# Moving the streamed weights' five places into a pool of their own, ahead of the working tiles

## The chip, the cores and the metric

The kernel runs on one NeuronCore of one Trainium2 chip. The metric is the device time of the whole program in microseconds (us), as the median of several runs; the profile is one further execution, taken by the hardware profiler.

## The reference

One layer of a hybrid decoder trunk over 4,096 tokens of width 1,024, in float32. One projection of the tokens gives 28 groups of 128 columns for five branches and a gate; the gated branches go through an output projection, and a layer norm closes the layer:

```python
proj = x @ w_in
xa, ba, ca, u, v, xc, da, dg, q, gate = jnp.split(proj, SPLIT_OFFSETS, axis=-1)
y_a = short_gated_conv(xa, ba, ca, conv_a_w)
y_b = spatial_gating(u, v, sg_ln_g, sg_ln_b, sg_w, sg_b)
y_c = multiscale_pool(xc, pool_w, pool_scale)
y_d = conformer_conv(da, dg, cc_dw_w, cc_dw_b, cc_ln_g, cc_ln_b, cc_pw_w)
y_e = memory_cross_attention(q, mem, w_kv)
h = jnp.concatenate([y_a, y_b, y_c, y_d, y_e], axis=-1) * jax.nn.silu(gate)
x = layer_norm(DEEPNORM_ALPHA * x + h @ w_out, ln_g, ln_b)
```

## The kernel before

**Order of the work.** The 4,096 tokens are eight blocks of 512, taken as four pairs (the loop over `p`). For a pair, `x_prep` (L121) loads the transposed tokens and makes seven combinations of the pair's x quarters, each in two halves of the contraction; each is split by `split_to` (L85) into a rounded high part (ScalarE) and the rest (VectorE), since every large product is done as three products of float32r splits. Then fourteen calls of `mpair` (L225) each make two groups of 128 columns for both blocks by seven half-size products, a Strassen scheme. One such product, `product` (L205), is 12 matmuls: four chunks of the contraction, and for each the three lines L209 (w high by x low), L211 (w low by x high) and L212 (w high by x high). The weights are the stationary operand, 128 by 128, the x tile the moving one, 128 by 512. The results are combined by VectorE (L90) and ScalarE (L236), and between the calls the branches' work is issued: convolutions, pooling, norms, attention. The 31-tap convolution of a pair (L462) is spread by `take(conv, ...)` over the first calls of the next pair.

**The streamed weights.** Each of the seven weight combinations of a call is a tile of 1,024 float32 a partition (both splits of half the contraction), taken with tag "ws": 5 places of 4,096 bytes. In the first pair `w_first` makes them and stores them to DRAM (L184); in the other pairs `w_again` (L199) loads them again (L202), 512 KB each, by the SyncE queue. `ready(5)` (L217) keeps five places in use: one is read, four are ahead. A load waits until the product before has freed its place.

**The output projection.** After the last pair, the split output weights `wo` and the norm's rows take 22 of the 28 places of the x tiles. `load_h` (L713) brings the gated branches for a unit of 256 tokens and splits them into five stationary tiles named h. For an even unit all five lie in x places; for an odd unit the first four lie in "ws" places and the fifth in an x place:

```python
        def part(j):
            if u % 2 == 0 or j == 4:
                return xc.tile([P, 2 * T], F32R, tag=htags[j if u % 2 == 0 else 5], name=nm("h"))
            return tt("ws", F32R, n="h")
```

A unit is two groups of 128 tokens, each 60 matmuls at L757 (10 chunks, 3 split products, 2 halves of the columns), so 120 matmuls; there are 16 units. Of an odd unit's 120 matmuls, 96 read a stationary tile in a "ws" place. VectorE adds the residual, takes the statistics and applies the norm (L760 to L770).

**The memory.** The pools lie one behind the other in each partition's memory, in the order in which they are opened. In the compiled kernel before: constants (`cp`) from byte 1,152; the 28 places of 4,096 bytes of the x tiles (`xc`) from 19,712 to 134,400; the working tiles (`tp`) from 134,400; small tiles (`sp`) from 225,664. Within `tp` the tags stand in the order of their first use: cc (8 × 2,048 bytes), raw (4 × 4,096), big (5 × 4,224), ss (2 × 2,048), ws (5 × 4,096, from 192,384 to 212,864), wk (4 × 2,176), st (2 × 2,048). The pointwise weights of the conformer branch, two tiles of `cp`, lie at 2,272 and 4,320; they are the stationary tiles of the matmuls at L485 to L487.

Of the kernel before, what the change touches and what calls it, by code (L numbers as in the profile page):

```python
# [18 lines left out]
P = 128  # L19
# [33 lines left out]
def trunk(ctx, tc, a, out):  # L53
    nc = tc.nc
    cp = ctx.enter_context(tc.tile_pool(name="cp", bufs=1))
    xc = ctx.enter_context(tc.tile_pool(name="xc", bufs=1))
    tp = ctx.enter_context(tc.tile_pool(name="tp", bufs=4))
    sp = ctx.enter_context(tc.tile_pool(name="sp", bufs=4))
    pm = ctx.enter_context(tc.tile_pool(name="pm", bufs=4, space=bass.MemoryType.PSUM))
# [4 lines left out]
    def nm(s):  # L64
        uid[0] += 1
        return f"{s}_{uid[0]}"
# [4 lines left out]

    def tt(tag, dt=F32, n=None):
        cols, bufs = SLOTS[tag]
        return tp.tile([P, cols], dt, tag=tag, name=nm(n or tag), bufs=bufs)

    def const(shape, src=None, dt=F32):
        t = cp.tile(shape, dt, name=nm("c"), tag=nm("ct"))
# [43 lines left out]
    def x_prep(p):  # L121
# [8 lines left out]
        def load(kap, j, n):  # L130
            tag = "big" if p == 0 and kap == 1 else "raw"
            raw = tt(tag, n="xraw")[:, :2 * T].rearrange("p (k t) -> p k t", k=2)
            k0 = 4 * j + 2 * kap
            nc.sync.dma_start(out=raw, in_=a["xT"][:, k0:k0 + 2, (2 * p + n) * T:(2 * p + n + 1) * T])
            raws[kap, j, n] = raw
# [32 lines left out]
    def w_first(mp, raws=None):  # L168

        m1, m2 = MPAIRS[mp]  # L170
        if raws is None:
            raws = []
            for m in (m1, m2):
                raw = tt("raw", n="wraw").rearrange("p (k c) -> p k c", k=NK)
                nc.sync.dma_start(out=raw, in_=a["w_in"][m])
                raws += [raw[:, :4], raw[:, 4:]]
        a11, a12, a21, a22 = raws
        s = tt("ss", n="ws0").rearrange("p (k c) -> p k c", k=4)

        def put(i, src):  # L180
            w = tt("ws", F32R, n="w")
            v = w.rearrange("p (s k c) -> p s k c", s=2, k=4)
            split_to(v[:, 0], v[:, 1], src)
            nc.sync.dma_start(out=wd[mp][i], in_=w.bitcast(F32))  # L184
            return v

        yield put(PA, a11)
        add(s, a21, a22)
        yield put(PT1, s)
        sub(s, s, a11)  # L190
        yield put(PT2, s)
        yield put(PB, a12)
        sub(a21, a11, a21)
        yield put(PT3, a21)
        sub(s, a12, s)
        yield put(PD, s)
        yield put(PT4, a22)
# [634 lines left out]
```

## Time and profile before

| | us |
|---|---|
| median of 3 runs | 1,802.05 |
| lowest, highest | 1,799.92, 1,803.36 |
| the profiled execution | 1,802.25 |
| its span, first to last instruction | 1,800.5 |
| mean granted TensorE clock in it | 0.992 of full |

The profile puts TensorE's matmuls (PE) and weight loads (PEld) in two rows, though one engine runs both; a matmul's end is modelled, and consecutive matmuls overlap in it, so their mean time is longer than the spacing of their starts. DVE is VectorE, ACT is ScalarE, POOL is GpSimd, SP is SyncE, whose queue (SPq) issues the DMAs. "L757" is line 757 of the kernel. A busy share is an average; which wait ends last in a stretch is read from the waits of that stretch.

### The profile page before, as it was taken

The numbers are of one execution on the slowest core, as the hardware profiler recorded it, in microseconds if no ns is written. First come the engines' busy times: TensorE is split into PE (matmuls) and PEld (weight loads), VectorE is DVE, ScalarE is ACT, GpSimd is POOL, SyncE is SP. The second block draws the span as 40 slices with busy tenths as digits, with TensorE's granted clock in tenths as the row PEclk, the third lists the DMA queues.
The fourth block names the chain that finished last, engine by engine and source line by source line (L and its number), as shares of the span: only waits on it lengthen the run. The fifth ranks groups of instructions, "written<-read, shape, count | busy, mean of one in ns | idle before, by whom it ended". The sixth has DMA issues, their size and how long they took to land.

```text
span 1800.5 us, 21764 instructions
## 1 busy us (share of the span) xinstructions
PE 1754.9 (97%) x7912; PEld 1383.6 (77%) x7912; DVE 1336.9 (74%) x2461; ACT 507.0 (28%) x937; POOL 44.8 (2%) x87
## 2 busy tenths in 40 slices
PE   5999999999999999999999999999989999999997
PEld 4887777878877787887778788777768888888786
DVE  8678887799966539997643999766379996665665
ACT  4323644420144423013532411354141010000300
POOL 0000000000100001010000000000000000000000
PEclk9999999999999999999999999999989999999999
DMA  7767455776744467675346766544683344332621
GB/s 276 274 239 261 183 198 196 280 238 208 235 163 137 133 217 270 201 230 177 129 151 211 269 201 213 197 143 141 205 289 99 119 132 141 127 100 79 213 71 47
DMA packets 128091, 332.79 MB, mean 185 GB/s; under 512 B 14064, under 2 KB 36080, under 8 KB 127984
## 3 DMA queue, kind: packets, MB, share of 16 engines
q1 hardware_dynamic: 127984, 331.39, 54.3%
q8 instruction: 63, 1.03, 0.2%
q14 instruction: 44, 0.36, 0.1%
HBM read 238.02 MB, written 93.32 MB: 184 GB/s over the span
## 4 chain that ended last, share of the span: by engine, by line
PE 91%; DVE 5%; DMA 2%; ACT 1%; issue 1%; SPq 0%; DVEq 0%; ACTq 0%
PE mm L757 24%; PE mm L209 19%; PE mm L212 19%; PE mm L211 19%; PE ax L632 3%; PE ax L607 2%; DVE xl L87 2%; PE ax L627 2%; DMA xraw<-in_xT 1%; DVE xraw L93 1%; PE ax L577 1%; PE ax L428 1%; PE ax L485 0%; PE ax L475 0%; PE ax L487 0%
## 5 line engine op out<-in xcount | busy, mean ns | idle before, releaser
L209 PE MATMUL mm<-xl,w 128*128 128x512 f32 x1568 | 627.4, 400 | 25.9 <-DVE xl L87 20.3
L211 PE MATMUL mm<-xh,w 128*128 128x512 f32 x1568 | 624.6, 398 | 0.9 <-DVE w L87 0.9
L212 PE MATMUL mm<-xh,w 128*128 128x512 f32 x1568 | 623.2, 398 | 0.0
L757 PE MATMUL mm<-wo,h 128*128 128x512 f32 x1920 | 445.8, 394 | 7.8 <-DVE h L87 7.8
L757 PEld LDWEIGHTS mm<-wo,h 128*128 128x128 f32 x1920 | 362.6, 189 | 87.6 <-DVE h L87 8.6
L209 PEld LDWEIGHTS mm<-xl,w 128*128 128x128 f32 x1568 | 297.1, 189 | 98.6 <-DVE xl L87 24.4
L212 PEld LDWEIGHTS mm<-xh,w 128*128 128x128 f32 x1568 | 296.8, 189 | 70.6 <-issue 3.6
L211 PEld LDWEIGHTS mm<-xh,w 128*128 128x128 f32 x1568 | 297.2, 190 | 68.2 <-issue 2.4
L462 DVE SCALAR_TENSOR_TENSOR acc<-din,c,acc 128x1024 f32<-128x1024 f32 x240 | 303.8, 1279 | 0.6 <-ACT acc L459 0.2
L86 ACT CAST h<-hraw 128x1024 fp32r<-128x1024 f32 (+1 forms) x48 | 43.3, 910 | 319.8 <-PE mm L757 235.3
L90 DVE TENSOR_TENSOR cc<-mm,v 128x512 f32<-128x512 f32 x112 | 76.8, 688 | 68.8 <-PE mm L212 68.3
L760 DVE SCALAR_TENSOR_TENSOR r<-r,mm 128x512 f32<-128x512 f32 x64 | 43.5, 687 | 79.8 <-PE mm L757 79.7
L86 ACT CAST xh<-xraw 128x1024 fp32r<-128x1024 f32 x56 | 57.9, 1051 | 64.2 <-DVE xraw L93 41.5
L90 DVE TENSOR_TENSOR t<-mm,t 128x512 f32<-128x512 f32 x56 | 38.6, 689 | 49.9 <-PE mm L212 49.9
L87 DVE TENSOR_TENSOR xl<-xraw,xh 128x1024 fp32r<-128x1024 f32 x56 | 66.7, 1221 | 11.3 <-ACT xh L86 11.1
L388 ACT ACTIVATE cc<-cc 128x512 f32<-128x512 f32 x44 | 27.9, 634 | 157.2 <-DVE cc L90 157.0
L87 DVE TENSOR_TENSOR h<-hraw,h 128x1024 fp32r<-128x1024 f32 (+1 forms) x48 | 49.7, 1041 | 26.3 <-issue 13.1
L236 ACT COPY t<-mm 128x512 f32<-128x512 f32 x56 | 32.9, 587 | 128.6 <-PE mm L212 128.5
L611 DVE TENSOR_REDUCE mx<-ax 128x2 f32<-128x512 f32 x64 | 42.7, 682 | 30.2 <-PE ax L607 29.9
L90 DVE TENSOR_TENSOR cc<-mm,t 128x512 f32<-128x512 f32 x56 | 38.5, 688 | 35.6 <-PE mm L212 35.1
L615 ACT ACTIVATE e<-ax,mx 128x256 f32<-128x256 f32 x128 | 59.3, 476 | 17.1 <-DVE mx L611 16.2
L435 ACT ACTIVATE nrm<-ax,nmr,rs 128x256 f32<-128x256 f32 x64 | 30.7, 570 | 115.9 <-DVE nmr L433 115.9
(147 smaller groups left out, 1531.8 us busy)
## 6 DMA issues: line engine op xcount, KB each, us to landing
w<-wd SPq DMA_DIRECT2D x294, 512.0 KB, 3.9
wd<-w SPq DMA_DIRECT2D x98, 512.0 KB, 2.9
xraw<-in_xT SPq DMA_DIRECT2D x32, 512.0 KB, 5.5
h<-cc SPq DMA_DIRECT2D x64, 256.0 KB, 3.1
hraw<-h SPq DMA_DIRECT2D x32, 512.0 KB, 4.1
r<-in_x SPq DMA_DIRECT2D x64, 256.0 KB, 3.0
out<-r SPq DMA_DIRECT2D x64, 256.0 KB, 2.0
wraw<-in_w_in SPq DMA_DIRECT2D x22, 512.0 KB, 4.3
```

The lines of the kernel that those rows point to most:

```text
L86: nc.scalar.copy(out=hi, in_=src)
L87: nc.vector.tensor_tensor(out=lo, in0=src, in1=hi.bitcast(F32), op=ALU.subtract)
L90: nc.vector.tensor_tensor(out=dst, in0=x, in1=y, op=ALU.add)
L209: nc.tensor.matmul(out=ps, lhsT=w[:, 0, k], rhs=xl[:, r], start=start and k == 0, stop=False, skip_group_check=True)
L211: nc.tensor.matmul(out=ps, lhsT=w[:, 1, k], rhs=xh[:, r], start=False, stop=False, skip_group_check=True)
L212: nc.tensor.matmul(out=ps, lhsT=w[:, 0, k], rhs=xh[:, r], start=False, stop=stop and k == 3, skip_group_check=True)
L462: nc.vector.scalar_tensor_tensor(out=accs[i], in0=dins[i][:, k:k + 2 * T], scalar=dww[:, i, k:k + 1], in1=accs[i], op0=ALU.mult, op1=ALU.add)
L611: nc.vector.tensor_reduce(out=mx, in_=sc[j], axis=AX.X, op=ALU.max, negate=True)
L615: nc.scalar.activation(out=e[:, c], in_=sc[j][:, c], func=AF.Exp, bias=mx[:, c:c + 1], accum_out=su[:, c:c + 1])
L632: nc.tensor.matmul(out=po[64 * j:64 * j + 64], lhsT=vm[:, mc, 64 * hd:64 * hd + 64], rhs=pT, start=(mc == 0), stop=(mc == 1))
L757: nc.tensor.matmul(out=ps[n], lhsT=l[:, P * (c % 2):P * (c % 2) + P], rhs=ww[:, T * n:T * n + T], start=(k == 0 and l is lo), stop=(k == N ...
L760: nc.vector.scalar_tensor_tensor(out=r[n], in0=r[n], scalar=ALPHA, in1=ps[n], op0=ALU.mult, op1=ALU.add)
```

## The change

The tag "ws" leaves the pool `tp` for a pool `wp`, opened between `xc` and `tp`. The tiles, their number, their size and the order of the instructions in the source stay as they are.

```diff
     xc = ctx.enter_context(tc.tile_pool(name="xc", bufs=1))
+    wp = ctx.enter_context(tc.tile_pool(name="wp", bufs=5))
     tp = ctx.enter_context(tc.tile_pool(name="tp", bufs=4))
...
     def tt(tag, dt=F32, n=None):
         cols, bufs = SLOTS[tag]
-        return tp.tile([P, cols], dt, tag=tag, name=nm(n or tag), bufs=bufs)
+        return (wp if tag == "ws" else tp).tile([P, cols], dt, tag=tag, name=nm(n or tag), bufs=bufs)
```

## Rows read from the trace of the kernel before

**Rows 1.** The page: span, and busy us (share of the span) of two engines.
```profile
span 1800.5 us, 21764 instructions
PE 1754.9 (97%) x7912; PEld 1383.6 (77%) x7912; DVE 1336.9 (74%) x2461; ACT 507.0 (28%) x937; POOL 44.8 (2%) x87
```

**Rows 2.** The page: the chain that ended last, share of the span by engine.
```profile
PE 91%; DVE 5%; DMA 2%; ACT 1%; issue 1%; SPq 0%; DVEq 0%; ACTq 0%
```

**Rows 3.** TensorE's waits: who waited for whom, us in total, times, longest.
```profile
PE mm L209 <- DVE xl L87: 20.3, 9, 7.6
PE mm L757 <- DVE h L87: 7.8, 2, 6.7
PE mm L209 <- DVE t L90: 4.8, 3, 3.4
```

**Rows 4.** Groups by line, 1395.5 to 1422.5 us (even unit): count | busy, mean ns | idle before.
```profile
L757 PE MATMUL mm<-wo,h 128*128 128x512 f32 x121 | 27.6, 389 | 0.0
L757 PEld LDWEIGHTS mm<-wo,h 128*128 128x128 f32 x120 | 22.5, 188 | 4.7
```

**Rows 5.** Groups by line, 1422.7 to 1449.7 us (the odd unit behind it).
```profile
L757 PE MATMUL mm<-wo,h 128*128 128x512 f32 x118 | 27.5, 394 | 0.0
L757 PEld LDWEIGHTS mm<-wo,h 128*128 128x128 f32 x117 | 22.0, 188 | 5.1
```

**Rows 6.** Windows, a later even unit and the odd one behind it (columns in rows 12).
```profile
1505.50:1532.50 27.00, 27.00 (x121) 22.37 (x120) 16.53 (x44) 3.79 (x4) 0.00 (x0) 1.00 0.40 130
1532.70:1559.70 27.00, 27.00 (x119) 21.95 (x118) 16.42 (x43) 1.67 (x2) 0.00 (x0) 1.00 0.37 116
```

**Rows 7.** Groups by line, PEld, 376 to 466 us (products of the second pair).
```profile
L212 PEld LDWEIGHTS mm<-xh,w 128*128 128x128 f32 x130 | 24.5, 188 | 5.8
L211 PEld LDWEIGHTS mm<-xh,w 128*128 128x128 f32 x129 | 24.3, 188 | 5.6
L209 PEld LDWEIGHTS mm<-xl,w 128*128 128x128 f32 x129 | 24.3, 188 | 5.7
```

**Rows 8.** Instructions of L486 (conformer's pointwise product): duration ns min/median/max, first and last start.
```profile
L486 PE MATMUL ax<-zz,c x32: 390/395/398, 507.3 to 1691.3; 128*128 128x512 f32 x32
```

**Rows 9.** The page's costliest groups: one of the product's three lines.
```profile
L209 PE MATMUL mm<-xl,w 128*128 128x512 f32 x1568 | 627.4, 400 | 25.9 <-DVE xl L87 20.3
```

**Rows 10.** Groups by line, 0 to 60 us: the same line.
```profile
L209 PE MATMUL mm<-xl,w 128*128 128x512 f32 x31 | 15.4, 495 | 16.7 <-DVE xl L87 13.3 <-DVE t L90 3.4
```

**Rows 11.** Windows: behind the first boundary between pairs, and at the second (columns in rows 12).
```profile
371.00:375.00 4.00, 4.00 (x12) 3.16 (x11) 2.70 (x3) 1.05 (x1) 0.00 (x0) 0.60 0.62 218
690.00:698.00 8.00, 6.49 (x27) 4.73 (x26) 8.00 (x8) 2.94 (x3) 0.00 (x0) 1.00 0.43 132
```

**Rows 12.** Windows: convolution stretches of the second to fourth pair, start of the output projection.
```profile
core 0: us, PE busy (x) PEld busy (x) DVE busy (x) ACT busy (x) POOL busy (x), PEclk, DMA share, GB/s
...
375.00:497.00 122.00, 122.00 (x527) 98.85 (x526) 118.12 (x134) 13.84 (x22) 10.55 (x14) 1.00 0.70 229
...
700.00:820.00 120.00, 120.00 (x522) 97.14 (x521) 115.77 (x134) 13.85 (x22) 10.28 (x14) 1.00 0.70 231
...
1024.00:1142.00 118.00, 118.00 (x510) 95.47 (x509) 114.45 (x130) 13.84 (x22) 10.54 (x14) 1.00 0.71 229
...
1338.00:1485.00 147.00, 147.00 (x632) 120.45 (x631) 144.78 (x267) 17.35 (x19) 0.00 (x0) 0.98 0.41 132
```

**Rows 13.** DMA issue of the streamed weights (KB, median us to landing), and SyncE's waits before it.
```profile
w<-wd SPq DMA_DIRECT2D x294, 512.0 KB, 3.9
...
SPq L202 <- PE mm L212: 661.7, 272, 9.6
```

## The prediction

> **What bounds the kernel now.** I read the page's busy table first, then the chain that ended last, then TensorE's waits, and last the spacing of its matmuls in stretches where it waits for nothing. TensorE is busy for 1,754.9 of the span's 1,800.5 us [rows 1], and 91% of the chain runs on it [rows 2]. Its three largest waits, all for VectorE, add up to 20.3 + 7.8 + 4.8 = 32.9 us, nearly all for the splits at the start and between pairs of blocks [rows 3]. So what counts is how fast matmul follows matmul, and the change can matter only there or in a wait that it makes longer.
>
> The spacing can be read from the weight loads: one LDWEIGHTS stands before each matmul, so its busy time and the idle time before it, added up and divided by the count, give one period. The output projection offers a clean comparison, because it goes through units of 120 matmuls whose stationary half-splits h lie by turns in two places: all in the pool of the x tiles for an even unit (`load_h`, L713), and for an odd unit four of five parts in the "ws" places. All else is the same. An even unit gives (22.5 + 4.7) / 120 = 226.7 ns [rows 4], an odd one (22.0 + 5.1) / 117 = 231.6 ns [rows 5]. Later units repeat it: 121 matmuls touch 27 us of an even one, 119 of an odd one, at full clock in both [rows 6]. Only 96 of an odd unit's 120 matmuls read a "ws" place, so one of those costs 226.7 + 4.9 × 120 / 96 = 232.8 ns. The products of the input projection, whose weights all stream through the "ws" places, give (24.5 + 5.8 + 24.3 + 5.6 + 24.3 + 5.7) / 388 = 232.5 ns [rows 7]: the same slow spacing. The LDWEIGHTS itself takes 188 ns everywhere; only the pause behind it grows, from 39 to 44 ns. So a stationary tile in a "ws" place costs TensorE about 5.8 ns a matmul, whatever the phase of the kernel.
>
> What is special about these places is their address. Before "ws", the pool tp holds 8 × 2,048 + 4 × 4,096 + 5 × 4,224 + 2 × 2,048 = 57,984 bytes, which is 226.5 × 256: the five "big" tiles of 4,224 bytes push "ws" 128 bytes off a multiple of 256, where the x pool's places lie. The places are also high, from 192,384 up, while the fast ones end at 134,400. Position off the multiple, or height: no row parts these two for sure. A third stationary tile speaks for the first: the pointwise weights of the conformer branch lie low (2,272 and up) but 224 bytes off, and their matmuls have the slow length, median 395 ns [rows 8], against 389 for the even units and 394 for the odd [rows 4, 5].
>
> **The change, part by part.** It adds, removes and reorders no instruction and no DMA. The pool wp is opened behind xc, so I expect the five places at 134,400 to 154,880: on a multiple of 256 like the x tiles, directly behind them. On either reading of the address this is the fast side, since 134,400 is a multiple of 256 and the height is next to the fastest places known. The tags cc, raw, big and ss move up by 20,480, which is 80 × 256, so they keep their position relative to 256; wk, st and the small pool stay where they are.
>
> Term 1, the products: 3 × 1,568 = 4,704 matmuls [rows 9]. In the first 60 us TensorE waits for splits and weights anyway; 3 × 31 of them are there [rows 10] and count nothing. That leaves 4,611 × (232.5 − 226.7) = 26.7 us. Term 2, the output projection: eight odd units × 120 × 4.9 ns = 4.7 us. Together 31.4 us.
>
> From this comes what other engines don't let through. Between pairs of blocks TensorE waits for x splits that VectorE works off without a break (8.00 of 8 us [rows 11]). TensorE comes there earlier by what it saves on the last two output groups, 168 matmuls × 5.8 ns = 1.0 us, while part of VectorE's chain starts earlier with it; I charge 0.7 us at three such places, 2.1 us. Then come three stretches in which VectorE is nearly full with the 31-tap convolution: it is busy for 118.1 of 122, 115.8 of 120 and 114.5 of 118 us [rows 12]. TensorE's gain there is about 525 × 5.8 ns = 3.0 us a stretch, and VectorE's room is 3.5 to 4.2 us, so it just fits; I charge 0.5 us each, and 0.5 us for the start of the output projection, where VectorE has 2.2 us of room in 147 us [rows 12] and TensorE gains about 1.5 us. That is 2.0 us. Net: 31.4 − 2.1 − 2.0 = 27.3 us.
>
> The streamed loads stay hidden: a transfer lands 3.9 us after its issue, and the queue's wait before it is for TensorE to free a place [rows 13]; four products of 12 × 226.7 ns lie between, 10.9 us, instead of 11.2. If that cover were gone a late load would cost up to its 3.9 us; it isn't. VectorE's and ScalarE's operands move too, at unchanged position relative to 256; I cost that at nothing, since neither engine is where the chain runs, and allow it 1 us either way in the range.
>
> The profiled execution took 1,802.25 us (span 1,800.5), and the median of the runs is 1,802.05; the sum is made against the first, 1,802.25 − 27.3 = 1,774.9, which against the median is 1,774.7. I take 1,774.8.
>
> A page speaks against all of this. The Trainium skill, "SBUF — State Buffer", section "Who interferes with whom", has the only contention in the lock of the port pair that VectorE and GpSimd share, gives TensorE two independent read ports, and says that "PE and ACT never wait on anyone". By that the place of a tile would be free, and the gain 0 instead of 27.3 us. The trace disagrees as far as the place goes: 226.7 against 231.6 ns between units that differ in nothing else.
>
> **The rivals.** (a) VectorE takes it back. Where it is nearly full, TensorE's gain turns into waits: the three convolution stretches lose 9.0 us and the start of the output projection 1.5, the boundaries 2.1. In addition the granted clock, whose mean was 0.60 in the 4 us after the waits of the first boundary but 1.00 at the second [rows 11], could fall at two more boundaries if their waits grow; 0.60 means 3.2 of the 4 us at the lower of its two levels, 1.2 instead of 2.4 GHz, which costs 1.6 us each time. The time is then 1,802 − 31.4 + 9.0 + 1.5 + 2.1 + 3.2 = 1,786.4. For it: the thin room. Against it: the room exists, and most of it is waiting for TensorE. (b) No change, 1,802: the pool lands elsewhere than I think, or what is slow is a height whose border lies below 154,880, or the streaming itself. Against the last: odd units are slow and stream nothing into these places. (c) Slower: at its new place the stream of transfers lands next to the x tiles, which no transfer writes today. If transfers there hold up TensorE's reads of the moving x tile by as much as the place does now, 5.8 ns, and the weights gain nothing, each product step goes to 238.3 ns and the time to 1,802 + 26.7 = 1,829; it decides from the point at which that cost is larger than the 5.8 ns gained. Against it: the slow spacing is the same in the products, with a DMA share of 0.70 [rows 12], as in odd units, with one of 0.37 [rows 6].
>
> **How the numbers follow.** The forecast, 1,768 to 1,781, has 0.70: its lower end is the full 31.4 us and some 2 us for uncertain spacing. Rival (a), 1,781 to 1,788, has 0.14, rival (b) 0.10, rival (c) 0.06. A range to 1,787 takes in the forecast and most of (a), about 0.82. A measurement of this kernel can tell about 0.2%, 3.6 us, from no change. Forecast and (a) are both faster by more than that: 0.84. Within it lies (b), 0.10, and above it (c), 0.06.
>
> **What the profile after would show.** Right: products and odd units at 226 to 227 ns by the weight loads' rows, matmul means of 389 ns, 121 matmuls in 27 us of every unit, and VectorE's idle time in the convolution stretches shrunk. For (a): the same spacing, but waits of TensorE for VectorE's adds or accumulators that weren't there. For (b): still 232 ns. For (c): spacing above 233 ns that follows the transfers' share. The prediction is wrong if the spacing falls and the time doesn't, or if the spacing stays.

## The result, and the profile after

The changed kernel takes **1,778.58 us**, the median of four runs (1,775.03 to 1,779.4), against 1,802.68 us for the kernel before in the same session (1,799.92 to 1,803.36). The ratio is 0.9865, with a 95% interval from 0.9848 to 0.9882: it is faster by 24.1 us, where 27.3 had been forecast. The profiled execution took 1,778.75 us, 23.5 less than the profiled one of before. In the compiled kernel the five places lie from 134,400 to 154,880, and cc, raw, big and ss have moved up by 20,480. TensorE's 7,912 instructions stand in the same order as before. Line numbers after L56 are one higher, so L209 is now L210 and L757 is L758.

The page of the changed kernel: span, busy time, the chain by engine, two of the costliest groups, and the issue of the streamed loads. They answer to [rows 1, 2, 9, 13].

```profile
span 1777.0 us, 21764 instructions
...
PE 1728.5 (97%) x7912; PEld 1379.6 (78%) x7912; DVE 1334.4 (75%) x2461; ACT 506.6 (29%) x937; POOL 46.2 (3%) x87
...
PE 87%; DVE 7%; DMA 3%; issue 1%; ACT 1%; SPq 0%; DVEq 0%; ACTq 0%
...
L210 PE MATMUL mm<-xl,w 128*128 128x512 f32 x1568 | 620.4, 396 | 27.5 <-DVE xl L88 21.3
...
L758 PE MATMUL mm<-wo,h 128*128 128x512 f32 x1920 | 439.8, 391 | 7.5 <-DVE h L88 7.5
...
w<-wd SPq DMA_DIRECT2D x294, 512.0 KB, 3.8
```

TensorE's busy time fell by 26.4 us with the same 7,912 matmuls, the span by 23.5. So nearly everything happened inside "busy": that row hides spacing, and a reader who looks for idle time only sees nothing. The loads land 3.8 us after their issue, against 3.9 before.

TensorE's waits in the changed kernel: us in total, times, longest; against [rows 3].

```profile
PE mm L210 <- DVE xl L88: 21.3, 12, 7.4
PE mm L758 <- DVE h L88: 7.5, 2, 6.8
PE mm L210 <- DVE t L91: 5.2, 3, 3.7
```

They add up to 34.0 us, where there were 32.9: 1.1 us more. Two waits that were not there before stand further down the list, 0.5 us for a transfer (L380) and 0.2 us for VectorE (L608).

Weight loads by line, 376 to 466 us, the products of the second pair; against [rows 7]. Columns: count | busy, mean ns | idle before.

```profile
L212 PEld LDWEIGHTS mm<-xh,w 128*128 128x128 f32 x133 | 25.0, 188 | 5.2
L213 PEld LDWEIGHTS mm<-xh,w 128*128 128x128 f32 x133 | 25.0, 188 | 5.1
L210 PEld LDWEIGHTS mm<-xl,w 128*128 128x128 f32 x132 | 24.8, 188 | 5.2
```

90 us now hold 398 of them instead of 388, and (25.0 + 5.2 + 25.0 + 5.1 + 24.8 + 5.2) / 398 = 226.9 ns, against 232.5. A load still takes 188 ns; the pause behind it is back to 39.

The odd unit from 1403.2 to 1430.2 us, by line; against [rows 5].

```profile
L758 PE MATMUL mm<-wo,h 128*128 128x512 f32 x121 | 27.6, 389 | 0.0
L758 PEld LDWEIGHTS mm<-wo,h 128*128 128x128 f32 x120 | 22.5, 188 | 4.7
```

This is, number for number, the even unit of before [rows 4]: the difference between the two kinds of unit is gone. Windows of the changed kernel: a later even unit and the odd one behind it [rows 6], then the convolution stretches and the start of the output projection [rows 12].

```profile
core 0: us, PE busy (x) PEld busy (x) DVE busy (x) ACT busy (x) POOL busy (x), PEclk, DMA share, GB/s
1484.80:1511.80 27.00, 27.00 (x121) 22.37 (x120) 16.54 (x44) 3.80 (x4) 0.00 (x0) 1.00 0.43 135
1512.00:1539.00 27.00, 27.00 (x121) 22.37 (x120) 16.82 (x44) 1.68 (x2) 0.00 (x0) 1.00 0.37 116
375.00:491.00 116.00, 116.00 (x514) 95.98 (x513) 114.52 (x130) 13.85 (x22) 11.23 (x14) 1.00 0.72 235
695.00:807.00 112.00, 112.00 (x496) 92.71 (x495) 110.63 (x127) 13.84 (x22) 10.37 (x14) 1.00 0.72 232
1013.00:1126.00 113.00, 113.00 (x500) 93.51 (x501) 111.61 (x127) 13.85 (x22) 11.22 (x14) 1.00 0.71 233
1322.00:1467.00 145.00, 145.00 (x639) 120.03 (x638) 143.89 (x269) 16.34 (x18) 0.00 (x0) 1.00 0.42 136
```

VectorE's idle time in the three convolution stretches has shrunk from 3.9, 4.2 and 3.6 us to 1.5, 1.4 and 1.4, and TensorE is busy throughout: its gain was paid out of VectorE's room, and the room was enough.

**Where the gain lies.** Matmul 1 of one trace is matmul 1 of the other, so the starts can be subtracted. The table sums the differences over stretches of calls (84 matmuls each); "steady" is 5.8 ns for every product, or 0.59 us for every odd unit, and "forecast" is that less the prediction's charges. The prediction counted 4,611 products, the rows here hold 4,620 behind the first call; the two sums are the prediction's.

| stretch | matmuls | steady | forecast | measured, us |
|---|---|---|---|---|
| first call of the first pair | 84 | 0 | 0 | −1.6 |
| its other thirteen calls | 1,092 | 6.3 | 6.3 | 5.1 |
| first call of pairs two to four | 252 | 1.5 | −0.6 | −1.1 |
| six calls behind it (convolution) | 1,512 | 8.8 | 7.3 | 8.4 |
| the other seven calls (attention and other branches between) | 1,764 | 10.2 | 10.2 | 6.7 |
| unit 0 of the output projection | 120 | 0 | −0.5 | 1.4 |
| units 1 to 15 | 1,800 | 4.7 | 4.7 | 4.6 |
| sum | 6,624 | 31.4 | 27.3 | 23.5 |

The convolution stretches and the units give what the spacing promised. The missing part lies where the branches' matmuls (attention's, spatial gating's, the conformer's) stand between the products, called the attention stretches below, and at the edges.

### The profile page after: what moved, and what is told of

Its sections match the earlier page's. It is cut to its first block, busy times and chain, and to the rows that moved or that the text cites. A ratio compares the mean times of both kernels' runs of the same rounds, so it can differ in the third digit from the quotient of the medians.

```text
span 1777.0 us, 21764 instructions
## 1 busy us (share of the span) xinstructions
PE 1728.5 (97%) x7912; PEld 1379.6 (78%) x7912; DVE 1334.4 (75%) x2461; ACT 506.6 (29%) x937; POOL 46.2 (3%) x87
## 4 chain that ended last, share of the span: by engine, by line
PE 87%; DVE 7%; DMA 3%; issue 1%; ACT 1%; SPq 0%; DVEq 0%; ACTq 0%
PE mm L758 24%; PE mm L210 18%; PE mm L213 18%; PE mm L212 18%; PE ax L633 3%; DVE xl L88 2%; PE ax L608 2%; PE ax L628 2%; DVE xraw L94 2%; DMA xraw<-in_xT 1%; PE ax L578 1%; PE ax L429 1%; DVE w L88 1%; PE ax L486 0%; PE ax L476 0%
## 5 line engine op out<-in xcount | busy, mean ns | idle before, releaser
L210 PE MATMUL mm<-xl,w 128*128 128x512 f32 x1568 | 620.4, 396 | 27.5 <-DVE xl L88 21.3
L212 PE MATMUL mm<-xh,w 128*128 128x512 f32 x1568 | 617.2, 394 | 0.9 <-DVE w L88 0.9
L213 PE MATMUL mm<-xh,w 128*128 128x512 f32 x1568 | 615.9, 393 | 0.0
L758 PE MATMUL mm<-wo,h 128*128 128x512 f32 x1920 | 439.8, 391 | 7.5 <-DVE h L88 7.5
L758 PEld LDWEIGHTS mm<-wo,h 128*128 128x128 f32 x1920 | 361.1, 188 | 82.9 <-DVE h L88 8.4
L210 PEld LDWEIGHTS mm<-xl,w 128*128 128x128 f32 x1568 | 296.2, 189 | 94.8 <-DVE xl L88 26.6
L237 ACT COPY t<-mm 128x512 f32<-128x512 f32 x56 | 32.9, 588 | 123.8 <-PE mm L213 123.7
L88 DVE TENSOR_TENSOR h<-hraw,h 128x1024 fp32r<-128x1024 f32 (+1 forms) x48 | 50.0, 1047 | 24.1 <-ACT h L87 13.3
L91 DVE TENSOR_TENSOR cc<-mm,t 128x512 f32<-128x512 f32 x56 | 38.5, 688 | 34.7 <-PE mm L213 34.2
```

What stands on the lines that cost most here:

```text
L88: nc.vector.tensor_tensor(out=lo, in0=src, in1=hi.bitcast(F32), op=ALU.subtract)
L91: nc.vector.tensor_tensor(out=dst, in0=x, in1=y, op=ALU.add)
L210: nc.tensor.matmul(out=ps, lhsT=w[:, 0, k], rhs=xl[:, r], start=start and k == 0, stop=False, skip_group_check=True)
L212: nc.tensor.matmul(out=ps, lhsT=w[:, 1, k], rhs=xh[:, r], start=False, stop=False, skip_group_check=True)
L213: nc.tensor.matmul(out=ps, lhsT=w[:, 0, k], rhs=xh[:, r], start=False, stop=stop and k == 3, skip_group_check=True)
L758: nc.tensor.matmul(out=ps[n], lhsT=l[:, P * (c % 2):P * (c % 2) + P], rhs=ww[:, T * n:T * n + T], start=(k == 0 and l is lo), stop=(k == N ...
```

## The experiments

All experiments change addresses alone: small tiles are put into a pool as padding, and each costs one extra GpSimd memset and nothing else in the order of the work. "w place" is a "ws" place.

**1. High, but on a multiple of 256** (e1_high_even). The prediction left open whether the old places were slow for their height or for their 128 bytes. Here they stay in `tp`, high up, and are pushed on to 192,512 = 752 × 256. The helper stands in the later experiments too, there with `wp` for `tp`:

```diff
+    def padding(name, floats):
+        nc.gpsimd.memset(tp.tile([P, floats], F32, tag=name, name=nm(name), bufs=1), 0.0)
...
         def put(i, src):
+            if mp == 0 and i == PA:
+                padding("pada", 32)
             w = tt("ws", F32R, n="w")
+            if mp == 0 and i == PA:
+                padding("padb", 32)
```

> The kernel before, with the five places of the streamed weights still high in the working pool (192,512 to 212,992) but on a multiple of 256 bytes. Theory P (what counts is the position relative to a multiple of 256): spacing of the products 226 to 227 ns, even and odd units of the output projection equal, time as the changed kernel's, 1,775 to 1,781 us. Theory H (what counts is the height in the partition): spacing stays 232 to 233 ns, odd units stay slower, time 1,799 to 1,805 us.

Measured: 1,776.96 us, ratio 0.986 (0.9837 to 0.9883). The weight loads of the same 90 us in this kernel, by line:

```profile
L219 PEld LDWEIGHTS mm<-xh,w 128*128 128x128 f32 x133 | 25.0, 188 | 5.1
L216 PEld LDWEIGHTS mm<-xl,w 128*128 128x128 f32 x133 | 25.0, 188 | 5.2
L218 PEld LDWEIGHTS mm<-xh,w 128*128 128x128 f32 x132 | 24.8, 188 | 5.2
```

90.3 / 398 = 226.9 ns, the changed kernel's spacing, without its pool. Height plays no part; 128 bytes do.

**2, 3, 4. Low, but off the multiple** (e2_low_off128, e3_low_off64, e6_low_off32). The counterpart: the changed kernel, with its five places in the low pool moved off by 128, 64 and 32 bytes. The diff is that for 128; for 64 the two pads have 16 and 48 floats, for 32 they have 8 and 56.

```diff
         def put(i, src):
+            if mp == 0 and i == PA:
+                padding("pada", 32)
             w = tt("ws", F32R, n="w")
+            if mp == 0 and i == PA:
+                padding("padb", 32)
```

> The changed kernel with its low places pushed 128 bytes off a multiple of 256 (134,528 up). Theory P: spacing 232 to 233 ns again, time 1,799 to 1,805 us. Theory H: spacing 226 to 227 ns, time 1,775 to 1,781 us.

> The changed kernel with its places pushed 64 bytes off a multiple of 256. Theory P with 256, or 128, as the unit: slow, 1,799 to 1,805 us, or another spacing above 227 ns. If the unit is 64 or less, so that only 128 off was special: 226 to 227 ns and 1,775 to 1,781 us. Theory H: 1,775 to 1,781 us too, but then the kernel with the low places 128 off is fast as well.

> The changed kernel with only the weights' places 32 bytes off. If any distance but 0 modulo 256 costs: spacing 230 to 236 ns, time 1,795 to 1,810 us. If a distance under 64 is free: 226 to 227 ns, 1,775 to 1,781 us.

Measured: 1,802.0 us at 128 bytes (ratio to the kernel before 1.0006, 0.9994 to 1.0017), 1,804.23 at 64 (1.0015, 1.0005 to 1.0025) and 1,804.19 at 32 (1.0012, 0.9999 to 1.0025). The whole gain is gone each time. The weight loads, 376 to 466 us, at 128 bytes:

```profile
L219 PEld LDWEIGHTS mm<-xh,w 128*128 128x128 f32 x130 | 24.5, 188 | 5.7
L220 PEld LDWEIGHTS mm<-xh,w 128*128 128x128 f32 x129 | 24.3, 188 | 5.7
L217 PEld LDWEIGHTS mm<-xl,w 128*128 128x128 f32 x129 | 24.3, 188 | 5.6
```

at 64 bytes:

```profile
L219 PEld LDWEIGHTS mm<-xh,w 128*128 128x128 f32 x129 | 24.3, 188 | 5.8
L220 PEld LDWEIGHTS mm<-xh,w 128*128 128x128 f32 x129 | 24.3, 188 | 5.8
L217 PEld LDWEIGHTS mm<-xl,w 128*128 128x128 f32 x129 | 24.2, 188 | 5.9
```

and at 32 bytes:

```profile
L219 PEld LDWEIGHTS mm<-xh,w 128*128 128x128 f32 x129 | 24.2, 188 | 5.8
L217 PEld LDWEIGHTS mm<-xl,w 128*128 128x128 f32 x129 | 24.2, 188 | 6.0
L220 PEld LDWEIGHTS mm<-xh,w 128*128 128x128 f32 x128 | 24.0, 188 | 5.8
```

The three lines together give 232.2, 233.3 and 233.2 ns. A smaller offset costs no less: against the changed kernel's 226.9, 32 and 64 bytes cost 6.3 and 6.4 ns a matmul, and 128 cost 5.3. So the pool as such does nothing; it worked because of where its first byte falls.

**5. The moving tile off the multiple** (e5_x_off128). Is it the stationary tile's own position that counts? Here the x places go to 128 bytes off (19,840), and the w places stay on a multiple (134,656 = 526 × 256).

```diff
+    nc.gpsimd.memset(xc.tile([P, 32], F32, tag="padx", name=nm("padx")), 0.0)
     def x_place(i, kap):
...
         def put(i, src):
+            if mp == 0 and i == PA:
+                padding("pada", 32)
```

> The changed kernel with the x tiles' places 128 bytes off and the weights' places on a multiple of 256. If only the stationary tile's position counts: products stay at 226 to 227 ns; even units of the output projection, whose stationary tiles lie in x places, slow to about 232.5 ns (27.9 us a unit), odd ones become the faster (24 of 120 slow); time 1,778.6 + 8 x 0.70 + 8 x 0.14 = about 1,785 us (1,782 to 1,788). If the moving tile's position counts too: products above 230 ns, time 1,800 us or more.

Measured: 1,801.06 us, ratio 0.9996 (0.9986 to 1.0006). Weight loads, 376 to 466 us:

```profile
L220 PEld LDWEIGHTS mm<-xh,w 128*128 128x128 f32 x130 | 24.5, 188 | 5.7
L219 PEld LDWEIGHTS mm<-xh,w 128*128 128x128 f32 x129 | 24.3, 188 | 5.7
L217 PEld LDWEIGHTS mm<-xl,w 128*128 128x128 f32 x129 | 24.3, 188 | 5.7
```

90.2 / 388 = 232.5 ns, slow, though the stationary tile lies on a multiple of 256. Its even unit from 1397.1 to 1424.1 us and its odd one from 1424.4 to 1451.4:

```profile
L765 PEld LDWEIGHTS mm<-wo,h 128*128 128x128 f32 x120 | 22.5, 188 | 4.7
```

```profile
L765 PEld LDWEIGHTS mm<-wo,h 128*128 128x128 f32 x118 | 22.2, 188 | 5.1
```

The even unit is fast at 226.7 ns, though here both its operands (h and wo, both in x places) are 128 bytes off. The odd unit is slow at 231.4, with h on a multiple in the w places and wo off. That is the reverse of a rule about one tile. What is left is a rule about two: the starts of the stationary and the moving tile must agree modulo 256. Within their tiles the operands of these matmuls start at multiples of 512 bytes, so the tiles' starts stand for theirs.

**6. Both off by the same 64 bytes** (e7_both_off64). This was made to part that rule of relative distance (R) from the one that both starts must lie on a multiple of 256 (B). The even unit of experiment 5 already speaks for R; here all products and units are put to it.

```diff
+    nc.gpsimd.memset(xc.tile([P, 16], F32, tag="padx", name=nm("padx")), 0.0)
     def x_place(i, kap):
...
             w = tt("ws", F32R, n="w")
+            if mp == 0 and i == PA:
+                padding("padb", 48)
```

> The changed kernel with the x tiles' places and the weights' places both 64 bytes off a multiple of 256. Theory R (what counts is the distance of the stationary tile's start from the moving tile's start, modulo 256): spacing 226 to 227 ns in products and in all units, time 1,775 to 1,781 us. Theory B (each of the two has to start on a multiple of 256): spacing 231 to 234 ns, time 1,800 us or more.

Measured: 1,775.84 us, ratio 0.9852 (0.9829 to 0.9874). Weight loads, 376 to 466 us:

```profile
L219 PEld LDWEIGHTS mm<-xh,w 128*128 128x128 f32 x133 | 25.0, 188 | 5.2
L220 PEld LDWEIGHTS mm<-xh,w 128*128 128x128 f32 x133 | 25.0, 188 | 5.2
L217 PEld LDWEIGHTS mm<-xl,w 128*128 128x128 f32 x132 | 24.8, 188 | 5.1
```

226.9 ns with no operand on a multiple. Only the distance counts. Its unit of measure is 256 and not 512: in experiment 1 the x places begin at 19,712 = 38.5 × 512 and the w places at 192,512 = 376 × 512, so there the distance is 256 modulo 512, and that was fast.

**7. More large tiles on a multiple** (e4_all_even). If position made the branches' matmuls slow as well, the rest of the memory would hold more to gain. Big becomes 4,352 bytes and wk 2,112, and one small constant moves ahead of the pointwise weights, which then lie at 2,304 and 4,352. The four wk places end up at 0, 64, 128 and 192 bytes off, so matmuls that read those are not part of this experiment.

```diff
-    SLOTS = {"ws": (2 * T, 5), "raw": (2 * T, 4), "big": (2 * T + 32, 5), "cc": (T, 8), "wk": (T + 32, 4),
+    SLOTS = {"ws": (2 * T, 5), "raw": (2 * T, 4), "big": (2 * T + 64, 5), "cc": (T, 8), "wk": (T + 16, 4),
...
+    sgg = const([P, 2])
     wpw = [const([P, 2, DG], dt=F32R) for _ in range(2)]
```

> The changed kernel with the other large stationary tiles moved onto a multiple of 256 as well: the five big tiles (queries, norms, accumulators, conformer splits) by 4,352 bytes each, the pointwise weights by moving one small constant ahead of them. Theory R: the 96 pointwise matmuls gain 5.8 ns each, 0.6 us; the 256 score matmuls change by less than 0.5 us. If the products between attention's matmuls are slow because of those tiles' distance, their spacing there falls to 226 to 227 ns and up to 4 us more are gained: 1,774 us. If the interruption itself slows them: 1,777 to 1,779 us, no difference that can be told from the changed kernel's.

Measured: 1,776.71 us, ratio 0.9868 (0.985 to 0.9885), against 0.9865 for the changed kernel beside it. The pointwise product in this kernel (min/median/max of duration):

```profile
L486 PE MATMUL ax<-zz,c x32: 387/396/500, 496.9 to 1666.8; 128*128 128x512 f32 x32
```

Its median is 396 ns, and was 395 [rows 8]. The pointwise matmuls of L486 to L488 come in groups of twelve between others. Of the eleven steps from start to start in a group, the first and the fourth are long, some 330 and 260 ns; the other nine average 231.8 ns here and 232.6 in the changed kernel, and only the last two are clearly shorter here (229.4 and 229.0, against 232.8 and 233.9). So in so short a group the position is worth next to nothing.

**8. The changed kernel again** (after_again), beside 6 and 7.

> The changed kernel itself, on the same chip as the kernel with all stationary tiles on a multiple of 256, for comparison: 1,775 to 1,781 us.

Measured: 1,776.91 us, ratio 0.9865 (0.9845 to 0.9884). No version beat the changed kernel by more than these intervals can tell.

## Why the prediction was right, and where it missed

**The mechanism held.** TensorE's spacing was the bound, the place of the weights set it, and both kinds of work that read "ws" places went from 232 to 227 ns [rows 5, 7]. Term 2 came out at 4.6 us for 4.7. The streamed loads stayed hidden, as costed. The Trainium skill's sentence in "SBUF — State Buffer", section "Who interferes with whom", that "PE and ACT never wait on anyone" is about one engine waiting for another. That a tile's place would then be free was the prediction's own step from it, and it doesn't hold here: experiment 1 changed the place alone and gained 25 us.

**The reading of the address was half right.** The prediction left height or a multiple of 256 open and leaned to the second. Height falls by experiment 1. "Off a multiple of 256" falls as a property of the stationary tile by experiments 5 and 6; it is the distance to the moving tile's start. The forecast needed no more, since x places and new w places both lie on multiples. The third witness, the pointwise weights at 395 ns [rows 8], was none: experiment 7 put them and their moving tiles on a multiple, and they stayed at 396.

**Term 1 is the step that failed in size.** It counted 4,611 products at 5.8 ns each, as if every product ran at the steady spacing. The next table has the spacing from start to start over the 4,116 products from the eighth call on (after 180 us). It takes the steps from one product to the next that are under 260 ns, 3,872 before and 3,868 after, and so leaves out waits and the first step behind other work, which is mostly 310 to 340 ns. The rank says how many such steps have followed one another without a break. Means in ns:

| rank | 1 to 4 | 5 to 8 | 9 to 12 | 13 to 16 | 17 to 20 |
|---|---|---|---|---|---|
| before | 231.9 | 233.2 | 232.7 | 232.0 | 233.3 |
| after | 231.7 | 228.8 | 227.3 | 226.8 | 226.6 |

So the equal distance is worth next to nothing in the first four steps, and the full 5 to 7 ns only from about the tenth on. In the changed kernel's order of time (start us, duration, then the instruction), after the spatial gating's matmuls at L578:

```profile
563.02 1.47 PE L578 MATMUL ax<-c,nrm 128*64 128x128 f32 x20
564.42 0.50 PE L213 MATMUL mm<-xh,w 128*128 128x512 f32 x1
564.76 0.40 PE L210 MATMUL mm<-xl,w 128*128 128x512 f32 x1
...
565.93 0.39 PE L213 MATMUL mm<-xh,w 128*128 128x512 f32 x1
...
568.22 0.39 PE L210 MATMUL mm<-xl,w 128*128 128x512 f32 x1
...
571.39 0.39 PE L213 MATMUL mm<-xh,w 128*128 128x512 f32 x1
```

From 564.76 to 565.93 there are five steps of 234 ns, then ten of 229 to 568.22, then fourteen of 226 to 571.39. In the attention stretches most runs of products are shorter than ten, and of the 4,116 products 248 are no such step: other work or a wait follows them, or they are the first behind other work. Those cost the term 248 × 5.8 = 1.4 us. The runs gained 19.8 us where 3,868 × 5.8 = 22.4 were counted, another 2.6. Together that is 4.0 us. The prediction's rows came from the convolution stretch, where a run goes on for 756 products, and were carried to stretches where runs are short.

That this comes close to the forecast's whole error in the profiled executions, 27.3 − 23.5 = 3.8 us, is partly luck. The steps into and among the other work took 1.3 us longer over the same part, a term that the prediction did not have and whose cause isn't shown, and the first call took 1.6 longer; against them stand the charges for the convolution stretches, which weren't used, and unit 0, which came out 1.9 better than charged.

**The charges.** For the convolution stretches 1.5 us was charged, and they fell short by 0.4 (8.8 − 8.4) with no wait of TensorE in them: VectorE's room was enough. The table above puts boundaries, first call and unit 0 at odd values, but they aren't the change's. Durations of the stretches in all ten profiled executions, in us, show it ("unequal" and "equal" are the distance of the two operands' starts modulo 256):

| stretch | five kernels at unequal distance | five at equal |
|---|---|---|
| calls 2 to 14 of the first pair | 299.1 to 300.2 | 294.0 to 294.3 |
| each convolution stretch | 118.0 to 118.5 | 115.2 |
| attention, second and third pair | 183.0 to 183.5 | 180.6 to 180.9 |
| units 1 to 15, to the end | 432.9 to 433.7 | 428.3 to 429.4 |
| first call | 56.1 to 57.6 | 55.5 to 57.7 |
| the three first calls of a pair, sum | 69.1 to 74.6 | 70.0 to 73.0 |
| unit 0 | 29.4 to 30.2 | 28.8 to 30.2 |

The upper four rows part cleanly; the lower three overlap, and their means differ by 0.3, 0.3 and 0.2 us. So of the 1.5 us that the boundaries' products should gain, 0.3 is left in these means; single executions scatter over 5 us there, so the charge of 1.2 us can't be told from the prediction's 2.1. What the two traces do show is that TensorE waited longer for VectorE there: 9.8 us over the three boundaries in the changed kernel, 8.4 before. This window of the changed kernel, at the second boundary, shows it against [rows 11] (columns as in the windows above):

```profile
682.00:690.00 8.00, 6.10 (x26) 4.54 (x25) 8.00 (x8) 2.60 (x3) 0.00 (x0) 1.00 0.42 129
```

VectorE still works without a break, and TensorE's busy time in such a window is 6.1 of 8 us. The 1.4 us of unit 0 is the granted clock's. The window of unit 0 before,

```profile
1337.50:1367.70 30.20, 30.20 (x121) 24.69 (x122) 29.50 (x39) 5.79 (x6) 0.00 (x0) 0.90 0.48 158
```

and after:

```profile
1320.00:1348.80 28.80, 28.79 (x121) 23.71 (x122) 27.80 (x35) 5.80 (x6) 0.00 (x0) 0.95 0.51 165
```

A mean of 0.90 over 30.2 us is 6.0 us at the lower level of 1.2 GHz, 0.95 over 28.8 us is 2.9; half of the difference is 1.6 us. In both kernels it follows TensorE's wait for h, and other executions at equal distance have 30.0 and 30.2 us there, so it isn't counted as gained.

**Readings that were off.** Three readings of the prediction are wrong, with little effect on its sum. The 168 matmuls behind its 1.0 us are two calls, so the last four output groups; the last two are 84 matmuls and 0.5 us. Of its 32.9 us of waits, the start and the boundaries' splits of x have 20.3; 7.8 are for the splits h of the output projection, and 4.8 for an add (L90). And transfers do write two x places, those of the norm's rows, once before the output projection.

**The rivals.** (a) VectorE takes it back, 1,786.4: the interval's upper end, 0.9882 × 1,802.68 = 1,781.4, lies below it, and the convolution stretches kept their gain. (b) No change: excluded by the interval. Its premises fall one by one: the pool lies at 134,400 as expected, height plays no part by experiment 1, and the streaming is the same in experiments 1 to 6, whose spacing is not. (c) Slower beside the x tiles: the spacing fell under the same transfers, DMA share 0.72.

**Left open.** No run shows why the distance matters: what TensorE reads together, and where the extra 5 to 6 ns arise, isn't seen in a trace. Distances other than 0, 32, 64, 128 and 256 weren't tried, nor other types than these float32r tiles. Nor is it shown whether the settling hangs on the count of matmuls or on time, 2 to 3 us here, nor whether one long step alone sets it back, as the pointwise groups of experiment 7 suggest: their two shorter steps are the sixth and seventh behind the long fourth.

## What to carry to other kernels

When TensorE has no idle time left, compare the spacing of its matmuls between stretches that differ in one thing; the even and odd units here showed 2% that no busy share or wait shows. Lay the stationary and the moving tiles of long matmul runs (float32r ones, as tried here) out so that their starts agree modulo 256 bytes, and read the compiled addresses: one tag of an odd size, five tiles of 4,224 bytes here, shifts all that is opened behind it. Multiply such a gain only by the matmuls that stand in long unbroken runs.

## What was not expected of the hardware

The pair of operands counts and not either tile: 226.9 ns at a distance of 0 modulo 256, also when both starts were 64 bytes off, against 232 to 233 at 32, 64 or 128. The smallest offset tried costs as much as any. And the fast spacing has to be regained after every interruption of the run, from 231.7 ns in the first four steps to 226.6 some twelve later, so runs of four or five show next to nothing of it.
